# First block of a two-block model on one Trainium2 core: S5's scan in a rotating frame, TensorE's order given by a list, two sets of HGRN2 decay buffers

## Chip, core and metric

One core of a Trainium2 chip (trn2) runs the whole program in one launch. The metric is the device time of one execution in microseconds. Engines are named as in the profile: PE is TensorE (PEld its weight loads), DVE is VectorE, ACT is ScalarE, POOL is GpSimd, SP is SyncE, which here issues nearly all DMAs.

## The reference

Two transformer-like blocks on 1024 tokens of 1024 features; only the first is touched. It normalises x, multiplies by `w_in`, and splits the columns among four mixers; the mixers' outputs are concatenated, multiplied by `w_out`, and a feed-forward layer follows:

```
a = rms_norm(x); proj = a @ w_in            # 25 blocks of 128 columns
S5:    bu = u @ B;  x[t] = A*x[t-1] + bu[t] # complex, diagonal A, 16 groups x 64 states
       y = gelu(Re(C x) + d*u); y = y * sigmoid(y @ w_glu); rms_norm
HGRN2: b = cumsum(log f) per chunk; scores[t,s] = sum_k q k exp(b[t]-b[s])  (s <= t)
       o = (q exp(b)) @ state + scores @ v; state = exp(b_last)*state + (k exp(b_last-b))^T v
FoX:   softmax attention with a forget-gate bias
mLSTM: causal conv over q,k; gated matrix memory, chunk by chunk
h = x + rms_norm(concat(y) @ w_out); h = h + ffn(rms_norm(h)); block 2 ...
```

## The kernel before

All of it stands in `block1a` and its helpers. `norm_T` normalises x and puts it transposed into SBUF as a high and a low part (`a_hi`, `a_lo`). A projection of 128 columns loads 512 KB of weights, splits them into `wh`, `wl` (ACT L67, DVE L69) and, for each half of the tokens, runs 8 x 3 matmuls of 128x512 into one PSUM tile `g_ps` (`mm3`, L91 to L93). I call the 24 matmuls of one half a half; 25 projections (24 of 128 columns and the 12 gate columns) are 50 halves. `to_fm` copies a half out (ACT) and writes it to DRAM; `to_tm` also transposes it on PE first (`g_tp`, L196, copied by DVE L281). The mixers read their inputs back from DRAM.

S5 (`s5_prep`, `s5_main`) folds 8 tokens into one row, so 128 steps are left for each of 8 state tiles t. For each t, PE forms the drive (`w_ps`, L460), ACT copies it, and a scan by doubling runs 7 rounds; a round is three DVE operations (L468, L470, L471) and a POOL copy, each waiting for the last. Then PE forms the output (`y_ps`, L477 and L479) and ACT applies gelu. After all t come transposes (`gT_ps`), the gate product (`glu_ps`, L497) and the norm.

HGRN2 (`hg_main`) works in four quarters of 256 tokens. A quarter's decays are a chain over ACT (logs and exponentials, L564 on), DVE, and POOL (L592, L593: 14 differences for each of two feature halves f into the tile `hlev`), then ACT's exponential of `hlev` (L594) and DVE's products (L598, L600). Each quarter has two chunks of 128 tokens: scores on PE (`sc_ps`, L638), a mask on DVE (`hP`, L641), then `d_ps`, `o_ps` (L642 to L647) and the state's increment `st_ps` (L651) on PE; DVE updates the state (L655), and the output is transposed back (`oT_ps`, L664) and normed. `hlev`, `z`, `q` and most other decay tiles have one buffer, so the next quarter's `hlev` can't be written until this quarter's scores have read it. The values `hvc` of a chunk (two loads by SP, L627) have two buffers.

mLSTM's preparation (`ml_prep`: convolution and gate rows, nearly all DVE) starts when HGRN2's SBUF tiles are released; then `ml_chunk` and `fox_tile` alternate for 8 tiles. `fox_prep` needs the space of the activations `a_hi`, `a_lo`, so it follows the last projection.

The order of every engine's queue is made by a planner when the program is built: it plays the program through with its own costs and puts on each engine the first ready instruction in program order. So before the change projections fill PE wherever the planner believed a mixer to be waiting, in the order of `block1a`: u, z and q of HGRN2, `hv`, then S5 and HGRN2, then gate, mLSTM's and FoX's columns. On the chip a queue is kept in that order. Pools give SBUF space as a stack, and a tile in reused space waits for the tiles that lay there.

Of the kernel before, what the change touches and what calls it, by code (L numbers as in the profile page):

```python
# [10 lines left out]
F32 = mybir.dt.float32  # L11
FR = mybir.dt.float32r
BF = mybir.dt.bfloat16
# [7 lines left out]
P = 128  # L21
T = 1024
# [13 lines left out]
class Kern:  # L36
    def __init__(self, ctx, tc, ins, out, dbg=None):
        self.ctx, self.tc, self.nc = ctx, tc, tc.nc
        self.i = ins
        self.out = out  # L40
        self.dbg = dbg or (lambda *a: None)
        self.raws = 2
        self.wring = None


# [155 lines left out]
    def block1a(self, x, ymix):  # L201

        nc, tc, i = self.nc, self.tc, self.i
        with ExitStack() as st:
# [16 lines left out]
            with ExitStack() as gem, ExitStack() as s5:  # L221
                right = lambda name, bufs=1: pool(name, bufs, stack=gem, side="right")
# [5 lines left out]
                self.s5p = pool("s5p", stack=s5)  # L228
                with ExitStack() as t_:
                    tmp = pool("n_tmp", stack=t_)  # L230

                    def load(t):
                        xt = tmp.tile([P, D], F32, tag="x", name="xt", bufs=8)
                        nc.sync.dma_start(xt, x[t * P:(t + 1) * P, :])
                        return xt
                    self.norm_T(self.sm, self.pst, load, 0, *a, lambda: tmp.tile([P, D], F32, tag="sq", name="n_sq"))
                    for j in range(2):
                        self.to_tm(j * P, self.d_u, j * P)
                    for j in range(2):
                        self.to_fm(512 + j * P, self.d_hz[j])  # L240
                        self.to_fm(256 + j * P, self.d_hq[j])
                    for j in range(4):
                        self.to_tm(768 + j * P, self.d_hv, j * P)
                    self.s5_prep(tmp)
                with ExitStack() as h_:
                    self.s5_main(pool("s5m", stack=h_))
                    self.hg_main(pool("hg", stack=h_))
                    self.gate_gemm()
                    for j in range(4):
                        self.to_fm(2052 + j * P, self.d_mqk[j])  # L250
                    for j in range(4):
                        self.to_tm(2564 + j * P, self.d_mv, j * P)
                    for j in range(2):
                        self.to_fm(1280 + j * P, self.d_fq[j])
                        self.to_fm(1536 + j * P, self.d_fk[j])
                        self.to_tm(1792 + j * P, self.d_fv, j * P)

            mp = pool("ml")
            with ExitStack() as t_:
                self.ml_prep(mp, pool("mlt", stack=t_))  # L260
# [6 lines left out]
    def to_fm(self, c0, dst):  # L267
# [6 lines left out]
        self.gemm_fm(self.i["w_in"], c0, consume)  # L274

    def to_tm(self, c0, dst, d0):
# [6 lines left out]
        self.gemm_tm(self.i["w_in"], c0, P, consume)  # L283

    def gate_gemm(self):
# [8 lines left out]
        gb = self.sm.tile([12, 1], F32, name="gbias")  # L294
        nc.sync.dma_start(gb, dap(self.i["gate_bias"], 0, [[1, 12], [1, 1]]))

        def consume(h, ps):
            o = self.stg.tile([P, 512], F32, tag="gs", name="gs")
            nc.vector.tensor_scalar(o[0:12], ps, gb, None, op0=ALU.add)
            nc.sync.dma_start(self.d_gate[:, h * 512:h * 512 + 512], o[0:12])  # L300
        self.gemm_halves(wh, wl, 12, consume)


    def s5_prep(self, tmp):
# [35 lines left out]
        pr = mx.tile([P, 8, 8], F32, name="s5pr")  # L340
        pi = mx.tile([P, 8, 8], F32, name="s5pi")
        pn = mx.tile([P, 8, 8], F32, name="s5pn")
# [13 lines left out]
        r, m = ar, ai  # L356
        for j in range(10):
            r2 = tt(tt(r, r, M), tt(m, m, M), S)
            m2 = tt(r, m, M)
            V.tensor_scalar(m2, m2, 2.0, None, op0=M)  # L360
            r, m = r2, m2
            if j >= 2:
                if j - 2 < 7:
                    V.tensor_copy(pr[:, :, j - 2], r)
                    V.tensor_copy(pi[:, :, j - 2], m)
                    V.tensor_scalar(pn[:, :, j - 2], m, -1.0, None, op0=M)
        self.s5pw = (pr, pi, pn)
# [40 lines left out]
        gs = sm.tile([16, 16, P], F32, name="s5gs")  # L408
        for g4 in range(4):
            ps = self.pss.tile([P, 512], F32, tag="s", name="g_ps")  # L410
# [16 lines left out]
        BL = self.s5BL = mx.tile([P, 8, 2, P], F32, name="s5BL")  # L427
        for t in range(0, 8, 2):
# [6 lines left out]
        for k in range(2):  # L435
            nc.sync.dma_start(self.s5wg[k], i["s5_w_glu"][0, k * P:(k + 1) * P])

    def s5_main(self, mx):
        nc, sm = self.nc, mx
        V = nc.vector  # L440
        M, A = ALU.mult, ALU.add
# [3 lines left out]
        for c in range(2):  # L445
            nc.gpsimd.tensor_copy(u2[:, 8 * c:8 * c + 8], u[:, :, P * c:P * c + P].rearrange("b i (g p) -> b g i p", p=16))
        ub = mx.tile([P, 16, P], F32, tag="u", name="s5ub")
        for g4 in range(4):
            ps = self.pst.tile([P, 4, P], F32, tag="t", name="ub_ps")
            for j in range(4):  # L450
                nc.tensor.transpose(ps[:, j], u2[:, 4 * g4 + j].rearrange("b i p -> b (i p)"), self.ident)
            nc.scalar.copy(ub[:, 4 * g4:4 * g4 + 4], ps)
        gt = mx.tile([P, 8, 256], F32, tag="u2", name="s5g")
        pr, pi, pn = self.s5pw
        CA = self.s5CA
        for t in range(8):
# [5 lines left out]
            X = [sm.tile([P, 2, P + 1], F32, tag=f"u{j}", name=f"s5x{j}", bufs=2) for j in range(2)]  # L462
            nc.scalar.copy(X[0][:, :, 1:], ps)
            for j in range(7):
                d = 1 << j
                a, b = X[j % 2], X[(j + 1) % 2]
                e = P + 1 - d
                V.scalar_tensor_tensor(b[:, :, 1 + d:], a[:, :, 1:e], pr[:, t, j:j + 1], a[:, :, 1 + d:], op0=M, op1=A)  # L468
                nc.gpsimd.tensor_copy(b[:, :, 1:1 + d], a[:, :, 1:1 + d])
                V.scalar_tensor_tensor(b[:, 0, 1 + d:], a[:, 1, 1:e], pn[:, t, j:j + 1], b[:, 0, 1 + d:], op0=M, op1=A)  # L470
                V.scalar_tensor_tensor(b[:, 1, 1 + d:], a[:, 0, 1:e], pi[:, t, j:j + 1], b[:, 1, 1 + d:], op0=M, op1=A)  # L471
            X = X[1]
            nc.gpsimd.memset(X[:, :, 0:1], 0.0)
# [11 lines left out]
        for k in range(2):  # L485
            for i4 in range(2):
                ps = self.pst.tile([P, 4, P], F32, tag="t", name="gT_ps")
                for j in range(4):
                    nc.tensor.transpose(ps[:, j], gt[:, 4 * i4 + j, k * P:(k + 1) * P], self.ident)
                nc.scalar.copy(gT[:, k, 4 * i4:4 * i4 + 4], ps)  # L490
        y2 = gt
        ss = sm.tile([P, 8], F32, name="s5ss")
        for i2 in range(4):
            ps = self.pst.tile([P, 2, 256], F32, tag="t", name="glu_ps")
            for j in range(2):
                for k in range(2):
                    nc.tensor.matmul(ps[:, j], gT[:, k, 2 * i2 + j], self.s5wg[k], start=(k == 0), stop=(k == 1))  # L497
            th = sm.tile([P, 2, 256], F32, tag="th", name="s5th", bufs=2)
# [3 lines left out]
            for j in range(2):  # L502
                nc.scalar.activation(th[:, j], y2[:, 2 * i2 + j], AF.Square, accum_out=ss[:, 2 * i2 + j:2 * i2 + j + 1])
        r = self.mean_rstd(sm, ss, 8, 256, 4 * EPS)
# [6 lines left out]
    def hg_main(self, mx):  # L511
# [3 lines left out]
        L = P  # L515

        for l in range(7):
            h = 64 >> l
            nc.sync.dma_start(dap(self.d_hvc, l * 256, [[h * 1792, 512 // h], [1792, h], [1, 256]]),
                              dap(self.d_hv, 0, [[2 * h * 512, 512 // h], [512, h], [1, 256]]))  # L520
# [33 lines left out]
        W2 = 256  # L554
        for qt in range(T // W2):
            s0 = slice(qt * W2, (qt + 1) * W2)
            z = mx.tile([P, 2, W2], F32, tag="z", name="hz")
            q = mx.tile([P, 2, W2], F32, tag="q", name="hq")
# [1567 lines left out]
```

## Time and profile before

| | |
|---|---|
| Median of 3 runs | 2963.76 us (2963.69 to 2968.23) |
| Profiled execution | 2964.78 us, its span 2963.1 us |
| Mean granted PE clock | 0.951 of full speed |
| PE / PEld / DVE / ACT / POOL busy | 91% / 76% / 62% / 42% / 23% of the span |

PE is the busiest engine over the whole span, but a mean over stages says little about this one. The stages of the first block are told apart by where their tiles appear in time: up to 47 us constants and the norm with the first projections; to 200 us projections; to 321 us S5 among projections; to 488 us HGRN2's chunks among projections; to 564 us the remaining projections, with mLSTM's preparation on DVE; to 590 us the start of mLSTM and FoX; to 716 us both together. `PEclk` is the granted clock as a share of 2.4 GHz: 0.5 is 1.2 GHz, and a value between is a mixture over the stretch.

### The profile page before, as it was taken

To read this page: it belongs to the slowest core of one execution; us is meant where nothing else is said; L and a number is where in the kernel's file an instruction comes from. 1 tells how busy PE (TensorE), PEld (TensorE's weight loads), DVE (VectorE), ACT (ScalarE), POOL (GpSimd) and SP (SyncE) were. 2 spreads that over 40 slices of the span, in tenths; PEclk is the share of its full clock that TensorE was granted. 3 is DMA by queue.
4 is the path that set the end of the run, shared out by engine and by line. 5 is a ranking of instruction groups with operands and counts; after the bars stand their busy time and mean duration, and the time that the engine had idled before them with its cause. 6 is when DMAs were issued, how large, how long until landed. Compare 5 with 4: busy or idle time off the path is not lost. (4 is left out here: it accounts for less than half of the span.)

```text
span 2963.1 us, 45158 instructions
## 1 busy us (share of the span) xinstructions
PE 2693.6 (91%) x16614; PEld 2252.8 (76%) x16631; DVE 1840.0 (62%) x4486; ACT 1235.7 (42%) x2379; POOL 693.3 (23%) x848
## 2 busy tenths in 40 slices
PE   5977878898999999899999999999999999799894
PEld 4855556687799978899887787888887888587683
DVE  5137666677688975988755263566655265776565
ACT  3124343254344465444654153344333122455553
POOL 6002221000267730577202000000000010332221
PEclk9988877899999999999999999999999999899997
DMA  4242222423232324432346252621113455699995
GB/s 120 72 138 68 64 76 88 136 81 112 94 114 86 112 89 136 135 115 86 107 136 172 65 158 57 154 74 45 47 40 120 167 178 171 204 308 314 297 302 209
DMA packets 336050, 388.65 MB, mean 131 GB/s; under 512 B 46962, under 2 KB 276220, under 8 KB 335684
## 3 DMA queue, kind: packets, MB, share of 16 engines
q1 hardware_dynamic: 322404, 355.65, 38.9%
q0 software_dynamic: 13280, 29.58, 3.6%
q8 instruction: 132, 2.16, 0.3%
q14 instruction: 90, 0.74, 0.1%
q10 hardware_dynamic: 144, 0.52, 0.0%
HBM read 326.83 MB, written 79.77 MB: 137 GB/s over the span
## 5 line engine op out<-in xcount | busy, mean ns | idle before, releaser
L69 DVE TENSOR_TENSOR f_w<-f_wr,f_w 128x512 fp32r<-128x512 f32 x264 | 293.8, 1139 | 54.6 <-ACT f_w L67 53.2
L91 PE MATMUL g_ps<-a_hi,wh 128*128 128x512 f32 (+1 forms) x648 | 269.6, 416 | 2.5 <-ACT wh L67 1.4
L92 PE MATMUL g_ps<-a_lo,wh 128*128 128x512 f32 (+1 forms) x648 | 265.6, 410 | 0.0
L93 PE MATMUL g_ps<-a_hi,wl 128*128 128x512 f32 (+1 forms) x648 | 263.2, 407 | 0.0
L67 ACT ACTIVATE f_w<-f_wr 128x512 fp32r<-128x512 f32 x264 | 158.9, 624 | 178.7 <-POOL f_wr L1080 58.0
L91 PE MATMUL f_ps<-t,f_w 128*128 128x256 f32 x704 | 202.9, 288 | 14.6 <-DVE c L1064 11.5
L93 PE MATMUL f_ps<-t,f_w 128*128 128x256 f32 x704 | 202.2, 288 | 7.5 <-DVE f_w L69 7.3
L92 PE MATMUL f_ps<-t,f_w 128*128 128x256 f32 x704 | 200.2, 284 | 0.0
L1314 ACT ACTIVATE at_sb<-at_sb,at_m 128x256 f32<-128x256 f32 (+7 forms) x224 | 142.3, 636 | 131.8 <-DVE at_m L1312 57.4
L69 DVE TENSOR_TENSOR wl<-wr,wh 128x1024 fp32r<-128x1024 f32 (+1 forms) x61 | 74.0, 1213 | 167.6 <-ACT wh L67 167.4
L1545 POOL TENSOR_TENSOR o<-o,on 128x256 f32<-128x256 f32 x32 | 24.6, 769 | 623.2 <-DVE at_z L1334 294.8
L91 PE MATMUL e_gps<-e_wh,e_xTh 128*128 128x256 f32 x528 | 152.8, 289 | 0.0
L91 PE MATMUL f_ps<-b,f_w 128*128 128x256 f32 x528 | 149.9, 284 | 2.6 <-ACT f_w L67 1.3
L93 PE MATMUL f_ps<-b,f_w 128*128 128x256 f32 x528 | 149.5, 284 | 2.1 <-DVE f_w L69 2.1
L91 PEld LDWEIGHTS f_ps<-t,f_w 128*128 128x128 f32 x704 | 135.9, 193 | 19.1 <-issue 15.1
L92 PE MATMUL e_gps<-e_wl,e_xTh 128*128 128x256 f32 x528 | 149.7, 284 | 0.0
L93 PE MATMUL e_gps<-e_wh,e_xTl 128*128 128x256 f32 x528 | 149.6, 283 | 0.0
L92 PE MATMUL f_ps<-b,f_w 128*128 128x256 f32 x528 | 149.3, 283 | 0.0
L91 PEld LDWEIGHTS g_ps<-a_hi,wh 128*128 128x128 f32 (+1 forms) x648 | 125.5, 194 | 27.6 <-ACT a_hi L72 1.7
L93 PEld LDWEIGHTS f_ps<-t,f_w 128*128 128x128 f32 x704 | 136.0, 193 | 11.4 <-DVE f_w L69 11.3
L93 PEld LDWEIGHTS g_ps<-a_hi,wl 128*128 128x128 f32 (+1 forms) x648 | 124.4, 192 | 25.5 <-issue 0.2
L92 PEld LDWEIGHTS g_ps<-a_lo,wh 128*128 128x128 f32 (+1 forms) x648 | 125.2, 193 | 24.2 <-issue 0.2
(668 smaller groups left out, 7786.7 us busy)
## 6 DMA issues: line engine op xcount, KB each, us to landing
e_wg<-in_w_gate_e_dram SPq DMA_DIRECT2D x33, 1024.0 KB
e_wu<-in_w_up_e_dram SPq DMA_DIRECT2D x33, 1024.0 KB
e_wd<-in_w_down_e_dram SPq DMA_DIRECT2D x33, 1024.0 KB
wr<-in_w_in_dram SPq DMA_DIRECT2D x60, 512.0 KB
f_dr<-in_w_ffn_down_dram SPq DMA_DIRECT2D x52, 512.0 KB
f_wr<-in_w_ffn_gate_dram SPq DMA_DIRECT2D x44, 512.0 KB
f_wr<-in_w_ffn_up_dram SPq DMA_DIRECT2D x44, 512.0 KB
Q<-qd SPq DMA_DIRECT2D x64, 256.0 KB
```

The costliest lines, as they stand in the source:

```text
L67: a = self.nc.scalar.activation(hi, raw, AF.Copy)
L69: return a, (eng or self.nc.vector).tensor_tensor(lo, raw, hi.bitcast(F32), ALU.subtract)
L91: nc.tensor.matmul(ps, lh, rh, start=(j == 0), stop=False)
L92: nc.tensor.matmul(ps, lh, rl, start=False, stop=False)
L93: self.last_mm = nc.tensor.matmul(ps, ll, rh, start=False, stop=(j == n - 1))
L1314: nc.scalar.activation(p, p, AF.Exp, bias=m[:, hd:hd + 1], accum_out=z[:, hd:hd + 1])
L1545: nc.gpsimd.tensor_tensor(o4, o4, on, A)
```

## The change

It touches `block1a` alone. **Order of PE.** `seq()` ties each PE instruction of its block behind the last PE instruction of the block before, so PE's queue follows a written list; the other engines are still planned. `gemms` is a generator that issues one half of a projection at each `next`; the transposes of a `to_tm` half now follow one half later. **List.** z and q of HGRN2 come first (first half of the tokens for all four, then the second), then u and `hv` with S5's preparation between; then S5, with a half after each step while the second-last list has any (5 of the 11 steps); the 30 halves of gate, mLSTM and FoX go 3 into S5's tail, 20 into HGRN2's 8 chunks (after the scores one, or two in an odd chunk, and one after the products), 6 into `ml_prep` and 1 behind it. **S5.** Multiplying by powers of the conjugate phase turns the complex recurrence into two real ones with the real factor mag^8, done by one scan instruction each; a table `E` of cosines and sines is built in `s5_prep` by doubling (42 DVE operations), with a renormalised squaring (`unit`, `square`). The copy of the drive by ACT goes; the output of t is formed two steps after its state. **HGRN2.** The first quarter's decays are issued before S5, the next quarter's when a quarter begins, in turn in the pools `hg` and `hg2`; `hg2` lies where S5's tiles were. Chunks are split into scores, products and output; the output of a chunk comes after the scores of the next. `d_ps`, `st_ps` and `o_ps` share one PSUM bank; `hvc` now has one buffer. The norm's discarded squares are written as bf16.

```diff
+    @contextmanager
+    def seq(self):
+        with self.tc.issue_after(self.pe_last) if self.pe_last else nullcontext():
+            yield
+        ins = self.nc.cur_bb.bb.instructions
+        self.pe_last = next(i for i in reversed(ins) if i.engine == mybir.EngineType.PE)
...
+                            norm(0)
+                            fm = [(512, self.d_hz[0]), (640, self.d_hz[1]), (256, self.d_hq[0]), (384, self.d_hq[1])]
+                            w = [self.load_w(self.ws, i["w_in"], fm[j][0], P, raw_bufs=self.raws, ring=early if j < 2 else None)
+                                 for j in range(4)]
+                            norm(1)
+                            prep = self.s5_prep(right("s5t", stack=p_))
+                            next(prep)
+                            for h in range(2):
+                                for j in range(4):
+                                    with self.seq():
+                                        self.gemm_half(w[j], P, h, self.keep_fm(fm[j][1]))
+                        hga = pool("hg", stack=hg_)
+                        self.hg_setup(hga)
+                        quarters = [self.hg_quarter(0, hga)]
+                        g = self.gemms([("tm", 128 * j, self.d_u, 128 * j) for j in range(2)]
+                                       + [("tm", 768 + 128 * j, self.d_hv, 128 * j) for j in range(4)])
+                        for _ in range(4):
+                            next(g)
+                        for _ in range(3):
+                            with self.seq():
+                                next(prep)
+                            next(g)
+                    s5m = right("s5m", stack=s5)
+                    for step in self.s5_steps(s5m):
+                        next(g, None)
...
+                    for step in self.s5_tail(s5m):
+                        next(g)
+                with ExitStack() as b_:
+                    hgb = right("hg2", stack=b_)
+                    for c in range(NT):
+                        if c % 2 == 0 and c // 2 + 1 < 4:
+                            quarters.append(self.hg_quarter(c // 2 + 1, hgb if c // 2 % 2 == 0 else hga))
+                        d = quarters[c // 2]
+                        with self.seq():
+                            self.hg_scores(d, c)
+                        if c:
+                            with self.seq():
+                                self.hg_out(quarters[(c - 1) // 2], c - 1)
+                        next(g)
+                        if c % 2:
+                            next(g)
+                        with self.seq():
+                            self.hg_products(d, c)
+                        next(g)
...
-        r, m = ar, ai
-        for j in range(10):
-            r2 = tt(tt(r, r, M), tt(m, m, M), S)
-            m2 = tt(r, m, M)
-            V.tensor_scalar(m2, m2, 2.0, None, op0=M)
...
+        E = self.s5E = mx.tile([P, 2, 8, P], F32, name="s5E")
+        for j in range(7):
+            d = 1 << j
+            c0, s0, c1, s1 = (E[:, a, :, x * d:x * d + d] for x in range(2) for a in range(2))
+            br, bm = (a[:, :, None].to_broadcast([P, 8, d]) for a in (r, m))
+            t_ = te[:, :, 0:d]
+            V.tensor_tensor(c1, c0, br, M)
+            V.tensor_tensor(t_, s0, bm, M)
+            V.tensor_tensor(c1, c1, t_, S)
+            V.tensor_tensor(s1, c0, bm, M)
+            V.tensor_tensor(t_, s0, br, M)
+            V.tensor_tensor(s1, s1, t_, A)
...
-            nc.scalar.copy(X[0][:, :, 1:], ps)
-            for j in range(7):
-                V.scalar_tensor_tensor(b[:, :, 1 + d:], a[:, :, 1:e], pr[:, t, j:j + 1], a[:, :, 1 + d:], op0=M, op1=A)
-                nc.gpsimd.tensor_copy(b[:, :, 1:1 + d], a[:, :, 1:1 + d])
...
+            cs, sn = E[:, 0, t, None, :].to_broadcast([P, 2, P]), E[:, 1, t]
+            V.tensor_tensor(v, ps, cs, M)
+            V.tensor_tensor(w[:, 0], ps[:, 1], sn, M)
+            V.tensor_tensor(w[:, 1], ps[:, 0], sn, M)
+            V.tensor_tensor(v[:, 0], v[:, 0], w[:, 0], A)
+            V.tensor_tensor(v[:, 1], v[:, 1], w[:, 1], S)
+            for c in range(2):
+                V.tensor_tensor_scan(w[:, c], self.s5m8[:, t:t + 1].to_broadcast([P, P]), v[:, c], 0.0, M, A)
+            G.memset(X[:, :, 0:1], 0.0)
+            G.tensor_tensor(X[:, :, 1:], w, cs, M)
+            G.tensor_tensor(v[:, 0], w[:, 1], sn, M)
+            G.tensor_tensor(v[:, 1], w[:, 0], sn, M)
+            G.tensor_tensor(X[:, 0, 1:], X[:, 0, 1:], v[:, 0], S)
+            G.tensor_tensor(X[:, 1, 1:], X[:, 1, 1:], v[:, 1], A)
...
+        for t in range(10):
+            if t >= 2:
+                with self.seq():
+                    outputs(t - 2, X.pop(t - 2))
+            if t < 8:
+                with self.seq():
+                    X[t] = states(t)
+            yield
```

## Rows read from the trace of the kernel before

**Rows 1.** Busy time by stage: stretch, each engine's busy us, PEclk, DMA.
```profile
47.00:200.00 153.00, 142.77 (x675) 109.61 (x674) 29.36 (x48) 22.37 (x33) 28.22 (x69) 0.97 0.33 96
200.00:321.00 121.00, 84.53 (x574) 65.21 (x573) 83.46 (x227) 53.52 (x92) 26.59 (x92) 0.82 0.26 71
321.00:488.00 167.00, 128.71 (x1069) 91.46 (x1067) 102.60 (x348) 61.60 (x106) 47.95 (x98) 0.70 0.24 64
488.00:564.00 76.00, 72.48 (x343) 59.26 (x344) 51.26 (x56) 29.80 (x36) 0.55 (x1) 0.98 0.35 114
564.00:590.00 26.00, 17.75 (x127) 14.86 (x124) 17.63 (x64) 8.84 (x19) 1.30 (x4) 0.75 0.90 239
590.00:716.00 126.00, 115.56 (x837) 97.68 (x837) 94.07 (x454) 62.11 (x146) 3.66 (x10) 0.96 0.20 62
```

**Rows 2.** The same for the instructions on the projections' PSUM tile g_ps alone.
```profile
47.00:564.00 517.00, 312.44 (x1226) 224.12 (x1226) 4.18 (x6) 27.10 (x47) 0.85 0.29 82
```

**Rows 3.** PE in order of time: two projection matmuls.
```profile
83.66 0.39 PE L91 MATMUL g_ps<-a_hi,wh 128*128 128x512 f32 x1
...
89.10 0.39 PE L91 MATMUL g_ps<-a_hi,wh 128*128 128x512 f32 x1
```

**Rows 4.** Waits of PE, 0 to 860 us: us in total, times, longest.
```profile
PE y_ps L479 <- DVE s5x L470: 25.7, 7, 13.4
PE sc_ps L638 <- DVE hlev L600: 17.9, 11, 5.2
...
PE o_ps L643 <- DVE hqe L606: 12.7, 2, 7.0
```

**Rows 5.** DVE in order of time: first and last operation of one S5 state.
```profile
203.25 0.49 DVE L468 SCALAR_TENSOR_TENSOR s5x<-s5x,s5pr 128x254 f32<-128x254 f32 x1 [12.00 <-ACT s5x L463]
...
211.25 0.28 DVE L471 SCALAR_TENSOR_TENSOR s5x<-s5x,s5pi,s5x 128x64 f32<-128x64 f32 x1
```

**Rows 6.** DVE by line, to 600 us: count, busy us, mean ns.
```profile
L579 DVE TENSOR_TENSOR_SCAN hb<-ones,ht 128x128 f32<-128x128 f32 x16 | 8.0, 508 | 0.0
...
L316 DVE TENSOR_TENSOR s5s<-s5s,s5s 128x8 f32<-128x8 f32 x30 | 4.6, 176 | 3.2 <-ACT s5s L338 2.6 <-ACT s5s L339 0.5
...
L575 DVE TENSOR_TENSOR ht<-ht,ht 128x512 f32<-128x512 f32 x4 | 2.8, 690 | 0.8 <-ACT ht L573 0.8
```

**Rows 7.** POOL by line, to 600 us, same columns.
```profile
L593 POOL TENSOR_TENSOR hlev<-hb 128x128 f32<-128x128 f32 x56 | 27.4, 489 | 0.0
```

**Rows 8.** DVE in order of time: a decay product while POOL works, and later.
```profile
403.55 0.48 DVE L600 TENSOR_TENSOR hlev<-hlev,hq 128x128 f32<-128x128 f32 x1
...
407.07 0.28 DVE L600 TENSOR_TENSOR hlev<-hlev,hq 128x128 f32<-128x128 f32 x1
```

**Rows 9.** POOL in order of time: a difference alone, and one beside DVE.
```profile
400.47 0.40 POOL L592 TENSOR_TENSOR hlev<-hb 128x128 f32<-128x128 f32 x1
...
403.44 0.44 POOL L593 TENSOR_TENSOR hlev<-hb 128x128 f32<-128x128 f32 x1
```

**Rows 10.** ACT in order of time: first operation of the last quarter's decays.
```profile
419.42 0.63 ACT L564 ACTIVATE ht<-hz 128x512 f32<-128x512 f32 x1
```

**Rows 11.** DVE in order of time: that quarter's last product.
```profile
458.52 0.41 DVE L614 TENSOR_TENSOR hke<-hke,hz 128x256 f32<-128x256 f32 x1
```

**Rows 12.** DVE in order of time: first and last operation of mLSTM's preparation.
```profile
495.86 0.75 DVE L701 TENSOR_SCALAR mqk<-mraw,vcol 128x1024 f32<-128x1024 f32 x1 [4.32 <-DMA mraw<-fm_mqk]
...
544.42 0.68 DVE L742 TENSOR_SCALAR frow<-frow 4x1024 f32<-4x1024 f32 x1
```

**Rows 13.** PE in order of time: last transposes, mLSTM's first, FoX's first.
```profile
563.69 0.66 PE L196 MATMUL g_tp<-ident,g_raw 128*128 128x128 f32 x4 [0.68 <-ACT g_raw L193]
564.18 0.38 PE L782 MATMUL mk_ps<-ident,mqk 128*128 128x128 f32 x2
...
589.36 0.47 PE L866 MATMUL at_s<-fkA,f_Q 128*128 128x128 f32 x1 [5.84 <-ACT f_Q L860]
```

**Rows 14.** Busy time, columns as in rows 1, while two loads of hvc land.
```profile
383.00:389.00 6.00, 0.00 (x0) 0.00 (x0) 1.00 0.85 208
```

More of the change, by code (lines that the diff above doesn't have):

```diff
@@ L265, in block1a, with gemm_half, gemms, flip @@
                 self.fox_tile(t)
-    def to_fm(self, c0, dst):
+    def gemm_half(self, w, n, h, consume):
+        ps = self.psg.tile([P, 512], F32, tag="g", name="g_ps")
+        self.mm3(ps[0:n], [(w[0][:, k, 0:n], w[1][:, k, 0:n], *self.a_half[h][k]) for k in range(KT)])
+        consume(h, ps[0:n])
+    def gemms(self, specs):
+        nc = self.nc
+        load = lambda sp: self.gate_w() if sp[0] == "gate" else self.gemm_w(self.i["w_in"], sp[1])
+        ahead = load(specs[0])
+        turn = []
+        def flip(h, ps, dst, d0):
+            raw = self.stg.tile([P, 512], F32, tag="gm", name="g_raw")
+            nc.scalar.copy(raw, ps)
+            def later():
+                tp = self.psg.tile([P, 4, P], F32, tag="g", name="g_tp")
+                for j in range(4):
+                    nc.tensor.transpose(tp[:, j], raw[:, j * P:(j + 1) * P], self.ident)
+                self.keep_tm(dst, d0)(4 * h, tp)
+            turn.append(later)
+        for j, sp in enumerate(specs):
+            w = ahead
+            if j + 1 < len(specs):
+                ahead = load(specs[j + 1])
+            for h in range(2):
+                now, turn[:] = list(turn), []
+                with self.seq():
+                    if sp[0] == "tm":
+                        self.gemm_half(w, P, h, partial(flip, dst=sp[2], d0=sp[3]))
+                    elif sp[0] == "fm":
+                        self.gemm_half(w, P, h, self.keep_fm(sp[2]))
+                    else:
+                        self.gemm_half(w, 12, h, self.keep_gate)
+                for t in now:
+                    with self.seq():
+                        t()
+                if turn and j + 1 == len(specs) and h == 1:
+                    with self.seq():
+                        turn.pop()()
+                yield
+    def keep_fm(self, dst):
         nc = self.nc
@@ L494, in s5_main @@
             ps = self.pst.tile([P, 2, 256], F32, tag="t", name="glu_ps")
[L495 to L498, printed above, removed]
+            with self.seq():
+                for j in range(2):
+                    for k in range(2):
+                        nc.tensor.matmul(ps[:, j], gT[:, k, 2 * i2 + j], self.s5wg[k], start=(k == 0), stop=(k == 1))
+            th = sm.tile([P, 2, 256], F32, tag="th", name="s5th")
             nc.scalar.activation(th, ps, AF.Tanh, scale=0.5)
@@ L514, in hg_main @@
         M, A, S = ALU.mult, ALU.add, ALU.subtract
[L515 to L520, printed above, removed]
+        self.hsm = sm
         lm = sm.tile([P, 7, 64], BF, name="hmask")
@@ new lines, in hg_scores @@
+    def hg_scores(self, d, c):
+        nc, sm = self.nc, self.hsm
+        V = nc.vector
+        M = ALU.mult
+        cc = c % (self.W2 // P)
+        lm, lev = self.hg[0], d["lev"]
+        vg = sm.tile([P, 512], F32, tag="v2", name="hvg", bufs=2)
+        nc.sync.dma_start(vg, self.d_hv[c * P:(c + 1) * P, :])
+        vc = sm.tile([P, 7, 2, HD], F32, tag="hvc", name="hvc")
+        for b_ in range(2):
+            nc.sync.dma_start(vc[64 * b_:64 * b_ + 64].rearrange("s l f d -> s (l f) d"),
+                              dap(self.d_hvc, c * 64 * 1792 + b_ * HD, [[1792, 64], [P, 14], [1, HD]]))
+        kT = sm.tile([P, 2, P], F32, tag="u0", name="hkT", bufs=2)
+        ps = self.pst.tile([P, 2, P], F32, tag="t", name="kT_ps")
+        for f in range(2):
+            nc.tensor.transpose(ps[:, f], d["ke"][f][:, cc], self.ident)
+        nc.scalar.copy(kT, ps)
+        pms = []
+        for f in range(2):
+            sc = self.pss.tile([P, 7, 64], F32, tag="s", name="sc_ps")
+            for l in range(7):
+                for b_ in range(2):
+                    pq = slice(64 * b_, 64 * b_ + 64)
+                    nc.tensor.matmul(sc[pq, l], *[lev[f][pq, l, a, 64 * cc:64 * cc + 64] for a in range(2)],
+                                     start=True, stop=True)
+            pm = sm.tile([P, 7, 64], F32, tag="hP", name="hP", bufs=2)
+            V.tensor_tensor(pm, sc, lm, M)
+            pms.append(pm)
+        d[c] = vg, vc, kT, pms
@@ L743, in ml_prep @@
         nc.sync.dma_start(self.d_fF, Ff)
+        for _ in range(6):
+            next(g, None)
         cols = sm.tile([P, 4, NT, 4], F32, name="mcols")
```

434 lines of the change are left out of this document (234 added, 200 removed).

## The prediction

> **What bounds the kernel now.** I read the page's slices first: PE is busy nine tenths of the span, but the first block has slices with PE at 6 or 7 and a granted clock below full. Then the busy time by stage, because an average over the block would hide which recurrence costs what. Here the reader should multiply PE's busy time by the clock, which gives its work at full speed [rows 1]: 142.77 x 0.97 = 138 us of 153, 84.53 x 0.82 = 69 of 121, 128.71 x 0.70 = 90 of 167, 72.48 x 0.98 = 71 of 76. From 47 to 564 us that is 369 us of work in 517 us: 148 us are lost, 15 in the projections, 52 beside S5, 77 in HGRN2 and 5 at the end. An upper limit on the work is what this is, as a busy PE also holds the tails of matmuls; the 1226 matmuls of the projections [rows 2], less S5's 64 on a tile of the same name, take 1162 x 5.44/24 = 263 us of it at the pitch of one half [rows 3]. So PE is the bound wherever it has work it may start, and the loss is waiting plus what it costs in clock: 0.70 in HGRN2's stage is a mixture of 1.2 and 2.4 GHz.
>
> The waits of PE name the places [rows 4]: S5's output on DVE's scan (25.7 us), HGRN2's scores on the products that make `hlev` (17.9), its output on `hqe` (12.7). These sum to 56 us, so most of the 148 isn't a wait at a semaphore but matmuls at half rate after one, and recurrence work queued in small groups. DVE's order of time shows why S5 waits: one state takes from 203.25 to 211.5 us, 8.3 us in seven rounds [rows 5]. For HGRN2 a quarter's decays run from 419.42 to 458.9 us, 39 us from the first ACT operation to the last product [rows 10, 11], and they end after the quarter before has freed its only `hlev`.
>
> **The change part by part.** I sum what is still lost between 47 us and mLSTM's first matmul, now at 564.18 [rows 13], since the work of PE stays (the same matmuls and transposes, in another order).
>
> *Start.* S5's preparation drops 71 DVE operations of about 0.18 us and gains 99 such, plus 42 for the table E: six of each of seven widths from 8 to 512 elements, between 0.18 and 0.69 us [rows 6], about 2.1 us a set, 12.7 us. Net 17.5 us more on DVE, which has 29 us of work in the 153 us to 200 [rows 1]; that slack hides it, and E isn't needed before S5's first state. If the planner puts it ahead of the norm's evictions, PE pays it all: 0 to 17, I take 4. The drive of S5 now needs u back from DRAM in space that the preparation frees late; 0 to 6 behind one half of cover, I take 3. Together 7.
>
> *S5.* A state now costs DVE one product of 256 columns out of PSUM (between a 128- and a 512-wide one, 0.28 and 0.69 [rows 6, 8], I take 0.42), four operations at 0.28 and two scans at 0.51 [rows 6]: 2.5 us in place of 8.3. POOL gets five operations, four of 128 at 0.49 [rows 7] and one of twice that, 2.9 us, which did only small copies before. DVE, POOL and PE work on neighbouring t, so a step takes the longest, 2.9, and a little for the hops: 3.2 us. Five of the eleven steps have a half of 5.44 us behind them, which hides the chain. Six have none: 19 us, with 8 us of PE work in them, so 11 lost, 4 for the last state's way through DVE, POOL and PE, 5 for matmuls at 1.2 GHz during and after. 20 us; without clock loss and at DVE's 2.5 us a step it would be 8, at twice the step 40.
>
> *HGRN2.* A chunk holds 2.5 halves (13.6 us) and, by my estimate, 6 us of its own matmuls: of the 369 - 263 = 106 us that aren't projections, S5, its preparation and the transposes take about half, and 48 remain for eight chunks. Two chunks and the half before them are 45 us, against 39 us for a quarter's decays [rows 10, 11], which can now start while the last quarter is used. So the decays just fit, and between scores and products stands 5.4 or 10.9 us for DVE's mask. `hvc` loses its second buffer: two loads kept the DMA engines 0.85 busy over 6 us [rows 14], in a window of at least one half and the next scores, 8 us. That is hidden with 2 us to spare; without the cover it is 6 us a chunk. I take 10 us lost over the eight chunks, with 0 if all fits and 45 if three quarters come 15 us late. This is the main gain: 77 goes to 10.
>
> *Preparation of mLSTM.* Its DVE work spans 495.86 to 545.1 us, after 4.3 us of waiting for a load: 53.5 us [rows 12]. Before, PE had 72 us of work in that stage [rows 1]. The list leaves seven halves, 38 us, and 2 us of transposes. So 14 us of PE are bare, and 3 for the clock: 17; 8 if the loads find their space early, 30 if DVE is also late with HGRN2's output.
>
> The projections' order, the later transposes of `to_tm` and the bf16 squares I cost at nothing: PE has the next half meanwhile. SP issues the same loads and stores, in another order.
>
> *Sum.* 7 + 20 + 10 + 17 = 54 us lost where 148 are: mLSTM begins 94 us sooner. Beyond that point FoX waits for the last projection: 563.69 to 589.36 is 26 us [rows 13], in which PE did 17.75 x 0.75 = 13 us on mLSTM [rows 1]. Now the last projection ends 14 us before mLSTM begins instead of with it, so FoX starts 14 us sooner still, with some 7 us of mLSTM left over for the stage that PE fills at 0.96. I keep 4 of the 7 net: 98 us. The profiled execution took 2964.78, 1.0 more than the median: 2964.8 - 98 - 1 = 2866 us. With all lower bounds (16 lost) it is 132 + 6 = 138 us and 2825; with all upper ones (17 + 6 + 40 + 45 + 30 = 138) 10 us and 2953.
>
> **The rivals.** *POOL and DVE in each other's way.* A product of DVE takes 0.48 us while POOL works on its differences and 0.28 after [rows 8]; POOL's difference goes from 0.40 to 0.44 [rows 9]. S5's states now put long operations on both at once. If the two took strict turns, a step would be DVE's four operations with both inputs in SBUF, 1.6 us, plus POOL's 2.9: 4.5 in place of 3.2, six times, 8 us more: 2874. The Trainium skill (SBUF — State Buffer, Who interferes with whom) says just that: the two share one port pair under an exclusive lock. By that rule the loser waits for the other's whole instruction; the rows agree in direction, but DVE's 0.20 more is half of a POOL operation, and POOL hardly slows.
>
> *The ends show.* Both bare places at their upper bounds, S5's tail 40 and mLSTM's preparation 30, 33 us more: 2899. For it: DVE is what both wait on, and it has the quarter's decays beside. Against: DVE is busy only 83 of 121 and 103 of 167 us there now [rows 1], with 8 x 8.3 = 66 us of scan to drop for 20.
>
> *The second set doesn't work.* `hg2` lies on S5's tiles and the planner may still issue a quarter's decays after the chunk before; then HGRN2's 77 us stay, 67 more: 2933. For it: POOL and DVE are queues, and one decay that waits holds what stands behind. Against: the tiles no longer force it.
>
> *The list starves PE (slower).* In a planned queue a stalled product has projections in front; in a written one everything stands behind it. The place is `hg_products`: its mask waits on DVE, perhaps behind the 28 products of a quarter's `hlev`. If each of the eight chunks idles and then runs at half clock, 98 + 10 us are eaten at 13.5 us a chunk, and from there the change is slower; at 15 us it is 2866 + 110 = 2976. For it: the longest single waits are 5 to 7 us in HGRN2 [rows 4], yet its stage loses 77: waits are paid several times over in clock. Against: one half stands in each gap.
>
> **How the numbers follow.** Forecast 0.44; turns of POOL and DVE 0.12; the ends 0.16; the second set 0.12; starved 0.08; all bounds kind (about 2830) 0.08. 0.2% is 5.9 us, about what a measurement here can tell from no change. Faster holds all but the starved case and a little of the second set's upper end: 0.89; the same 0.03; slower 0.08. The range must reach from the kind case, most of it, to past the second set: 2830 to 2938, which leaves out the starved case and the edges, some 0.15.
>
> **What would show it.** Right: no POOL copy and no round of three in S5, a step of about 3 us; PE's clock near 1 from 47 us to the end of HGRN2 except in S5's last six steps; waits of the scores on `hlev` gone; mLSTM's first matmul near 470 us, with PE idle 10 to 20 us before it behind the gate rows. Wrong: waits of `o_ps` on the mask or on `hvc` in every chunk, a clock of 0.7 in HGRN2's stage, or a start of S5 much after 137 us, which is 47 + 13.4 halves (15 less those done) + 17 us for preparation and transposes.

## The result, and the profile after

| | before | changed |
|---|---|---|
| Median of 4 runs | 2965.99 us (2963.69 to 2968.75) | 2927.55 us (2922.52 to 2931.43) |
| Profiled execution | 2964.78 us | 2922.52 us, its span 2920.8 us |
| Mean granted PE clock | 0.951 | 0.957 |

The ratio is 0.9869 (95% interval 0.9849 to 0.9889): 38 us faster, inside the stated range of 2830 to 2938, but 61 us above the forecast of 2866, which had promised 98. mLSTM's first matmul came at 513.98 us and not near 470. The stages after, with bounds at the same events as before (S5's first transposes, HGRN2's first chunk, its last output, mLSTM's first matmul, the end of FoX); columns as in [rows 1]:

```profile
47.00:162.60 115.60, 91.29 (x447) 73.00 (x445) 59.38 (x161) 31.27 (x47) 44.32 (x101) 0.92 0.28 72
162.60:255.08 92.48, 87.94 (x440) 66.01 (x441) 28.24 (x83) 22.39 (x54) 21.17 (x47) 0.88 0.27 80
255.08:451.39 196.31, 170.20 (x1570) 142.67 (x1569) 116.42 (x335) 73.79 (x117) 44.55 (x95) 0.90 0.36 100
451.39:513.98 62.59, 47.98 (x221) 39.34 (x220) 50.02 (x68) 26.15 (x31) 1.59 (x4) 0.84 0.30 94
513.98:669.21 155.23, 138.80 (x931) 117.25 (x929) 105.42 (x497) 62.91 (x151) 4.98 (x14) 0.84 0.30 89
```

Length less busy time times clock, as in the prediction, gives what each stage lost: 31.6 us up to S5, 15.1 in S5, 43.1 in HGRN2 and 22.3 in mLSTM's preparation, 112 in all, where the forecast had 7, 20, 10 and 17. The measure is rough: HGRN2's 1570 matmuls count 153 us of work here and 162 in the run below with all orders mended, so 8 or 9 of its 43 us are the measure. What PE waited for between 47 and 520 us (columns as in [rows 4]):

```profile
PE o_ps L834 <- ACT hkT L805: 14.4, 2, 7.4
PE oT_ps L860 <- ACT hoS L847: 9.9, 1, 9.9
PE mc_ps L947 <- ACT mrow L923: 9.2, 1, 9.2
PE g_tp L341 <- ACT g_raw L336: 9.1, 3, 7.9
PE ub_ps L581 <- POOL s5u L575: 8.9, 1, 8.9
PE g_ps L100 <- ACT wh L76: 6.4, 1, 6.4
```

The old waits, on S5's scan, `hlev` and `hqe`, are gone. In their place PE waits for short copies on ACT, and a copy of 0.35 us can't take 7 us. What stood ahead of it shows on ACT in order of time (start, duration, line, operation, idle before and its releaser), in the third chunk of HGRN2; below it the instruction of PE that waited:

```profile
314.54 1.70 ACT L765 ACTIVATE hlev<-hlev 128x1792 f32<-128x1792 f32 x1 [4.62 <-POOL hlev L764]
316.15 0.57 ACT L370 COPY gs<-g_ps 128x512 f32<-128x512 f32 x1
320.04 1.70 ACT L765 ACTIVATE hlev<-hlev 128x1792 f32<-128x1792 f32 x1 [3.32 <-POOL hlev L764]
321.64 0.40 ACT L784 ACTIVATE hke<-hke 128x256 f32<-128x256 f32 x1
321.95 0.35 ACT L805 COPY hkT<-kT_ps 128x256 f32<-128x256 f32 x1
```
```profile
322.35 0.70 PE L834 MATMUL o_ps<-hvg,hkT 128*64 128x64 f32 x8 [6.98 <-ACT hkT L805]
```

The exponentials of the next quarter's `hlev` stand ahead of this chunk's `hkT`, and both wait for POOL's differences, the first and last of which are:

```profile
308.28 0.43 POOL L763 TENSOR_TENSOR hlev<-hb 128x128 f32<-128x128 f32 x1 [0.36 <-DVE hb L750]
...
319.56 0.44 POOL L764 TENSOR_TENSOR hlev<-hb 128x128 f32<-128x128 f32 x1
```

PE, which by the list may do nothing else, goes on with its products at 322.35, 7 us late, and needs 7.4 us for the rest of them, which takes 3.1 in the chunk before: 1.8 us more of waiting, for the mask, and a granted clock of 0.50 from 322.35 to 329.71. The next quarter's decays ended at 325 us; the scores that need them came at 359.4.

Ahead of S5 the same happens with quarter 0. DVE's copy of a mask waits for POOL, which makes the mask only after S5's tables; the weights' split on ACT stands behind the decays that stand behind that copy; later u's `g_raw` stands behind the exponentials; and S5's read of u is issued on SP behind the stores of `hv`. DVE, PE and SP in order of time:

```profile
85.83 0.27 DVE L693 COPY hmask<-hmask 64x448 bf16<-64x448 bf16 x1 [12.22 <-POOL hmask L691]
```
```profile
91.94 0.79 PE L100 MATMUL g_ps<-a_hi,wh 128*128 128x512 f32 x1 [6.42 <-ACT wh L76]
112.74 1.12 PE L341 MATMUL g_tp<-ident,g_raw 128*128 128x128 f32 x4 [7.87 <-ACT g_raw L336]
162.60 3.80 PE L581 MATMUL ub_ps<-ident,s5u 128*128 128x128 f32 x16 [8.87 <-POOL s5u L575]
```
```profile
147.49 7.37 SPq L380 DMA_DIRECT2D tm_hv<-gs  x2
155.50 0.62 SPq L572 DMA_DIRECT2D s5u<-tm_u  x1
```

### The profile page after: what moved, and what is told of

Its sections match the earlier page's. It is cut to its first block, busy times and chain, and to the rows that moved or that the text cites. A ratio compares the mean times of both kernels' runs of the same rounds, so it can differ in the third digit from the quotient of the medians.

```text
span 2920.8 us, 45015 instructions
## 1 busy us (share of the span) xinstructions
PE 2665.4 (91%) x16614; PEld 2252.0 (77%) x16631; DVE 1835.7 (63%) x4446; ACT 1221.4 (42%) x2361; POOL 698.4 (24%) x832
## 5 line engine op out<-in xcount | busy, mean ns | idle before, releaser
L100 PE MATMUL f_ps<-t,f_w 128*128 128x256 f32 x704 | 203.1, 289 | 15.5 <-DVE c L1262 12.6
L100 PEld LDWEIGHTS f_ps<-t,f_w 128*128 128x128 f32 x704 | 136.6, 194 | 19.7 <-issue 16.2
L102 PEld LDWEIGHTS f_ps<-t,f_w 128*128 128x128 f32 x704 | 136.6, 194 | 9.2 <-DVE f_w L78 9.1
```

Source lines behind the costliest of these rows:

```text
L100: nc.tensor.matmul(ps, lh, rh, start=(j == 0), stop=False)
L102: self.last_mm = nc.tensor.matmul(ps, ll, rh, start=False, stop=(j == n - 1))
```

## The experiments

Ratios are to the kernel before on the same chip, with 95% intervals; the changed kernel is 0.9869. 0.001 is 3 us.

**The exponentials behind the copies.** `levels` holds L765 to L771; `act_last()` is here the copy `hoS`.

```diff
                             self.hg_products(d, c)
+                        if c % 2 == 0 and c // 2 + 1 < 4:
+                            with tc.issue_after(self.act_last()):
+                                quarters[c // 2 + 1]["levels"]()
```

> The changed kernel with one difference in order: in quarters 1 to 3 of HGRN2 the two exponentials of hlev on ACT, and the products behind them, are issued behind the copy hoS of the running chunk; POOL's 28 differences stay where they are. Theory A (ACT's queue: the exponentials, put early by the planner, wait for POOL's differences and hold the copies hkT and hoS that PE needs): the three waits of PE in HGRN2's stage (9.9, 7.0 and 7.4 us) go with the half clock behind them, the stage falls from 196 to about 165 us and the time from 2927.6 to about 2895. Rival B (a quarter's decays are simply too long beside two chunks): the scores of the next quarter now wait for hlev, and the time stays within 6 us of 2927.6 or grows. Rival C (the clock stays low for another reason): the waits go but the clock of the stage stays at 0.90, and only about 24 us are won.

0.9783 (0.9766 to 0.9799), 25 us less than the changed kernel. HGRN2 took 171.3 us in place of 196.3, at a clock of 0.98:

```profile
257.78:429.06 171.28, 163.73 (x1570) 137.15 (x1569) 116.79 (x335) 72.82 (x117) 46.84 (x95) 0.98 0.41 114
```

Its waits on `hkT` are gone; one on `hoS`, of 6.7 us, is left, on a state update that stood on DVE behind a decay (L753 of that kernel) waiting for ACT. Only the exponentials and DVE's products behind them were moved, and POOL's differences kept their place, so theory A holds: not the length of a quarter's decays but their place in the queue was the cost.

**The start.** Three edits ahead of S5; `act_last()` is here the copy of u's third half.

```diff
-        V.tensor_copy(lm[64:128], lm[0:64])
+        G.tensor_copy(lm[64:128], lm[0:64])
...
+                                with tc.issue_after(self.act_last()):
+                                    quarters[0]["levels"]()
...
-        nc.sync.dma_start(u, self.d_u.rearrange("(b i) f -> b i f", i=8))
+        nc.gpsimd.dma_start(u, self.d_u.rearrange("(b i) f -> b i f", i=8))
```

> The changed kernel with three edits ahead of S5: the copy of HGRN2's mask is done by POOL instead of DVE; the exponentials of quarter 0's hlev are issued on ACT behind the copy of u's third half; S5's u is read back through POOL's queue instead of SP's. Theory A (queues in a fixed order hold PE's inputs behind HGRN2's early decays): the waits of PE of 6.4 us (wh) and 7.9 us (g_raw) go, that of 8.9 us on s5u falls to about 4, S5's transposes begin at about 140 instead of 162.6 us, and the time falls by about 20 to 2907. Rival B (S5's start is set by S5's own preparation on POOL and DVE): the transposes begin no earlier than 157 and the time stays within 6 us.

0.9763 (0.9745 to 0.9781), 31 us less. S5's transposes began at 137.03 in place of 162.60, the time that the prediction had worked out for a start without loss, and from 47 us to there PE lost 2 us. What each of the three edits brought isn't separated:

```profile
47.00:137.03 90.03, 88.12 (x448) 71.53 (x447) 57.58 (x161) 31.70 (x47) 48.28 (x102) 1.00 0.33 89
```

**The halves of mLSTM's preparation first.** The loop of six halves in `ml_prep` moves from behind the gate rows to ahead of them.

> The changed kernel with one move: the six halves of ml_prep are issued in the program ahead of the gate rows instead of behind them. Theory A (the sixth half began, waited for its weights' low part, which stood on DVE behind the gate rows, and the transposes of the gate rows were queued inside it, so 46 of its and its successor's matmuls ran after them): the last projection ends near 493 us instead of 512, mLSTM's first matmul is near 500 instead of 514, FoX starts as much sooner, and the time falls by about 14 to 2913. Rival B (DVE's chain of 45 us from 458.9 is the bound whatever PE does): mLSTM begins no more than 4 us sooner and the time stays within 6 us.

0.9853 (0.9837 to 0.987), not told apart from the changed kernel. The last projection ended at 491 in place of 513, but mLSTM's gate columns were still complete only at 506.3 (498 in the changed kernel, which then had nearly two halves to do): DVE's chain takes some 45 us from 460 in either. Mostly rival B.

**One set of decay buffers.** `hgb` becomes `hga` in the list.

> The changed kernel with all quarters of HGRN2 in one set of decay buffers (hg2 is not used). A quarter's decays took 27 us in the changed kernel (255.8 to 282.5) and can now start only when the scores and products of the quarter before are done, with some 20 us of PE work up to the next scores. If the second set works (theory A): three waits of the scores on hlev of 7 to 15 us come, with half clock behind them, and the time grows by 20 to 45 us to 2948 to 2973. If it gives nothing because the copies on ACT are what PE waits for (rival B): within 6 us of 2927.6.

0.9912 (0.9896 to 0.9929), 13 us more: below theory A's 20, but not nothing. HGRN2 took 211 us. The waits on ACT's copies are gone from its rows, and the old ones are back:

```profile
PE sc_ps L812 <- DVE hlev L771: 22.5, 15, 5.9
PE kT_ps L804 <- DVE hke L785: 9.0, 3, 3.5
```

So the second set does what it says; it traded one wait for another.

**No list.** `seq()` yields without its tie.

> The changed kernel without the ties on PE: the same program, but TensorE's queue is ordered by the planner as on the other engines. Theory A (the list is worth something: it spreads the halves over S5 and HGRN2, and what was lost was lost to the other engines' queues): slower than the changed kernel by 15 to 40 us, ratio 0.992 to 1.000, with a clock near 0.8 or less in HGRN2's stage. Rival D (the list starves PE, as one of the rivals of the prediction had it: behind a stalled product everything stands): faster than the changed kernel by 10 us or more, ratio 0.9835 or less.

0.9766 (0.9747 to 0.9784): 30 us *faster* than with the list. I had expected the opposite. HGRN2 began at 237.5 us (255.1 in the changed kernel) and took 190.6 (196.3). Up to S5's transposes, S5, HGRN2:

```profile
47.00:174.21 127.21, 112.66 (x550) 90.78 (x549) 61.87 (x162) 34.74 (x52) 44.97 (x101) 0.95 0.29 76
174.21:237.47 63.26, 60.76 (x345) 42.84 (x343) 25.72 (x79) 18.31 (x49) 19.30 (x46) 0.97 0.26 80
237.47:428.03 190.56, 171.02 (x1564) 141.75 (x1563) 115.39 (x335) 71.81 (x116) 45.27 (x95) 0.93 0.39 108
```

The planner put whole halves in front of S5 and single projection matmuls between its steps. Three drives in a row there, 3.5 us apart at full clock (first fence), and those of the changed kernel's bare steps (steps with no half behind them), 3.1, 4.2 and 6.2 us apart:

```profile
201.06 0.66 PE L589 MATMUL w_ps<-s5ub,s5BL 128*64 128x128 f32 x8
204.65 0.66 PE L589 MATMUL w_ps<-s5ub,s5BL 128*64 128x128 f32 x8
208.06 0.66 PE L589 MATMUL w_ps<-s5ub,s5BL 128*64 128x128 f32 x8
```
```profile
206.75 0.66 PE L592 MATMUL w_ps<-s5ub,s5BL 128*64 128x128 f32 x8
209.88 0.66 PE L592 MATMUL w_ps<-s5ub,s5BL 128*64 128x128 f32 x8
214.09 0.66 PE L592 MATMUL w_ps<-s5ub,s5BL 128*64 128x128 f32 x8
220.25 1.12 PE L592 MATMUL w_ps<-s5ub,s5BL 128*64 128x128 f32 x8 [0.37 <-ACT s5g L621]
```

**S5's scan alone, in the kernel before.** The new table and states and outputs of S5 in the old `s5_prep` and `s5_main`, no list.

> The kernel before with the new S5 alone: table E and the rotating scan on DVE and POOL in place of the doubling rounds, outputs two steps later, nothing else of the change (to make room, hvc and the gate hth of HGRN2 have one buffer, the row of ones is one column, and S5's temporaries share a tag). Theory A (S5's scan was what PE waited for beside S5): the waits on s5x of 25.7 us go, a state takes about 3 us in place of 8.3, and the time falls by 15 to 30 us against the kernel before, ratio 0.990 to 0.995. Rival B (without a list the planner leaves S5 or HGRN2 bare in other places): ratio 0.998 or above.

1.0023 (1.0006 to 1.0039): nothing won. A state is short now, and S5's transposes of the output began at 250 in place of 312 us, HGRN2 ended at 446 in place of 485; yet mLSTM began at 564.5, as before:

```profile
201.80:257.11 55.31, 44.32 (x195) 33.05 (x194) 24.05 (x69) 30.46 (x45) 25.58 (x56) 0.57 0.17 48
257.11:446.00 188.89, 155.32 (x1291) 108.25 (x1291) 121.43 (x376) 76.29 (x134) 55.25 (x117) 0.74 0.26 74
446.00:564.50 118.50, 109.77 (x505) 88.31 (x505) 59.09 (x73) 36.46 (x46) 0.65 (x2) 0.97 0.32 100
```

The last row says where the gain went: the projections that had run beside the long scan were still to be done, 118 us of them, behind HGRN2. S5's stage (clock 0.57) and HGRN2's (0.74) still lost 30 and 74 us by the measure above. That smaller buffers in HGRN2 cost a part isn't excluded.

**All together.** The edits of the first three experiments, and a quarter's decays issued on ACT and DVE behind the chunk before (its copy `hoS` and its state update):

```diff
+                            with tc.issue_after(ends[0]) if c else nullcontext(), tc.issue_after(ends[1]) if c else nullcontext():
+                                quarters.append(self.hg_quarter(c // 2 + 1, ...
...
+                        ends = [self.last(e) for e in (mybir.EngineType.Activation, mybir.EngineType.DVE)]
```

> The changed kernel with the three edits together (exponentials of hlev behind hoS; the three edits ahead of S5; the halves of ml_prep ahead of the gate rows) and one more: a quarter's decays are issued on ACT and DVE behind the hoS copy and the state update of the chunk before, because with the first edit alone one wait of 6.7 us was left, on a state update that stood on DVE behind a decay that waited for ACT. Measured alone against the kernel before: ratios 0.9783, 0.9763, 0.9853, the changed kernel 0.9869. Theory A (each is a separate wait in a fixed queue): the gains add, 25 + 31 + 5 + 8 = 69 us less than the changed kernel, ratio 0.964, and no wait of PE in HGRN2's stage is over 2 us. Rival B (they share a bound behind them, DVE's chain in mLSTM's preparation): not more than 45 us less, ratio 0.972 or above.

0.9645 (0.9629 to 0.9661), 2857 us: the gains add, and no wait of PE in HGRN2's stage is over 2 us. Start, S5, HGRN2 and mLSTM's preparation:

```profile
47.00:137.50 90.50, 87.46 (x446) 71.18 (x445) 56.56 (x158) 27.89 (x42) 48.35 (x103) 1.00 0.33 89
137.50:230.62 93.12, 88.54 (x441) 66.46 (x441) 28.21 (x83) 22.21 (x54) 21.18 (x47) 0.87 0.29 82
230.62:397.61 166.99, 163.37 (x1570) 137.19 (x1569) 118.67 (x336) 66.48 (x114) 47.76 (x95) 0.99 0.43 117
397.61:453.11 55.50, 44.80 (x223) 37.15 (x222) 49.29 (x65) 28.83 (x35) 1.59 (x4) 0.90 0.41 116
```

**Halves moved from HGRN2 to S5**, on top of these edits (one list, a half behind all eleven steps, 13 in HGRN2, 7 in `ml_prep`).

> As e7_all, with the written list changed: one list of projections, a half behind each of the eleven S5 steps (five before), HGRN2's chunks get 13 halves in place of 20, ml_prep 7 in place of 6, one behind it as before. Theory A (six bare S5 steps lose about 14 us with their half clock, and mLSTM's preparation is DVE's chain, so a half moved into either place is free): about 15 us less than e7_all, ratio 0.959 if that one reaches 0.964. Rival B (a quarter's decays need some 33 us of two chunks, which then hold 33 us of PE work): scores wait for hlev or the output for ACT in three quarters, and it is no faster than e7_all.

0.9655 (0.9632 to 0.9678): no gain, rival B. S5 ran at a clock of 1.00 from 136.6 to 232 us, but HGRN2 with seven halves (40 us) less took 147.5 us, only 19.5 less, and waits on `hoS` (11.8 us in two) and on the mask (5.2) are back. A quarter then took 37 us (147.5/4); that its decays need as much is argued from this, not measured.

**Free on PE, with the edits of all together.** First all of PE, then S5's steps and tail alone; without its tie `seq()` only yields. The edit of the second, which ties PE again at HGRN2:

```diff
+                    self.tied = False
                     for step in self.s5_steps(s5m):
```

> e7_all without the ties on PE: the planner orders TensorE's queue, the four edits on ACT, DVE, POOL and SP's side stay. In e5_no_list S5 ran 177 to 214 us at full clock, with single projection matmuls between the steps, and a step took 3.4 us; in e7_all it ran 147 to 203 with six bare steps at half clock. Theory D (a whole half is too coarse a unit of cover; the planner's interleaving of single matmuls is worth 10 to 18 us even when the copies no longer wait): ratio 0.958 to 0.961. Rival A (once the copies on ACT no longer wait, the written list is as good): 0.9645 within 0.002, or slower, since HGRN2 in e7_all has no wait over 2 us and the planner put some there in e5_no_list.

> e7_all with the ties on PE lifted from S5's steps and tail alone (the halves issued there are free too); HGRN2 and all else stay tied. If the list's cost is the bare S5 steps and its gain is HGRN2's order, this is the best of the kernels: ratio 0.958 to 0.961, S5 without half clock and HGRN2 without a wait over 2 us. If free halves in S5 only move the bare place (behind the list in HGRN2 the same number of halves is left): 0.9645 within 0.002.

0.9614 (0.9596 to 0.9631) and 0.961 (0.9593 to 0.9626). The tie costs about 10 us in S5 and nothing that shows in HGRN2 once the copies don't wait.

**S5 free in the changed kernel.**

> The changed kernel with that one edit: the ties on PE lifted from S5's steps and tail, all else as changed. e5_no_list was 0.9766 against 0.9869; its profile had S5's gate products done 18 us sooner and HGRN2's end 6 us sooner still. If most of what the ties cost lies in S5 (the wait of 8.9 us on s5u and the bare steps): ratio 0.980 to 0.983, with HGRN2's three waits on ACT's copies as in the changed kernel. If it lies in HGRN2: 0.985 or above.

0.9825 (0.9809 to 0.9842), 13 us less. HGRN2 began at 237.7, as without any list (237.5), but took 203 us against 190.6: with the copies waiting, the tie cost there too.

**Two halves moved to mLSTM's preparation**, from the best of these (18 in HGRN2, 8 in `ml_prep`).

> e11_s5_free with two of HGRN2's 20 halves moved into ml_prep (8 in place of 6, one behind it as before). In e11 the projections ended at 430 us and mLSTM's preparation, bound by DVE's chain that begins when HGRN2 ends (391), left PE 15 us with little work and half clock until 450 and after. Theory A (that bare place is real, the halves in HGRN2 are not all needed): HGRN2 ends 11 us sooner, mLSTM begins 8 to 11 us sooner, ratio 0.957 to 0.958. Rival B (a quarter's decays need some 36 us of two chunks, and two quarters now have 36): scores or outputs wait again in two quarters, 5 to 10 us each, and the ratio stays at 0.961 within 0.002.

0.9597 (0.9577 to 0.9617), 2846.55 us: the lowest, not told apart from 0.961. mLSTM's gate columns came 8 us sooner (437 for 445), and FoX's end 9, though waits on the mask (6.3 us in three) came with it; 6 of the 9 were lost later in the program, where the runs don't say why.

## Why the prediction was wrong

The direction and the range held; the size was off by 61 us, and the sum by stage says where. Against the forecast, mLSTM began 44 us late: 24.6 at the start, 33.1 in HGRN2, 5.3 in its own preparation, less 4.9 in S5 and less 14 because the same work, counted as busy time times clock, came out smaller (355 for 369 us); those 14 are the measure, so the start and HGRN2 lost somewhat less than these terms say. Beyond mLSTM's start 15.5 us more went (11.5 lost where 4 were to be kept).

*Start, 4 + 3 us: this step failed.* Its first half had the size by luck: the first transposes of the norm came at 23.9 us instead of 17.95, and by 47 us PE was 3 us behind, but not because of table E, whose first operation ran at 33.58. SP now issues two loads of weights ahead of x, so x lands later and ACT squares it 4 us later (before; then changed); two more splits of weights on DVE, 1.22 us each, stand ahead of x's scaling:

```profile
8.25 1.06 ACT L104 ACTIVATE n_sq<-xt 128x1024 f32<-128x1024 f32 x1 [1.49 <-DMA xt<-in_x_dram]
```
```profile
12.29 1.06 ACT L113 ACTIVATE n_sq<-xt 128x1024 bf16<-128x1024 f32 x1 [0.36 <-DMA xt<-in_x_dram]
33.58 0.17 DVE L484 TENSOR_TENSOR s5E<-s5E,s5q 128x8 f32<-128x8 f32 x1
```

The second half was mis-sized because I asked only when S5's inputs come free. The new work in front of S5 that costs is quarter 0's decays: each of their waits on POOL holds ACT and DVE, and with these the weights and u. With the queues' order mended S5 began at 137.0, as computed. "SP issues the same loads and stores, in another order" was put at nothing, and both halves show it was not: the weights ahead of x, and u read behind the stores of `hv`.

*HGRN2, 10 us: this is the term that failed most.* "So the decays just fit" was right, with time to spare (325 for 359 us). The loss comes from a queue that the step never priced: ACT, which also carries `hkT`, `hoS`, `g_raw` and the weights, waits inside the decays for 28 differences of POOL, 12 us. Three quarters, three waits of 7 to 10 us, each with half clock behind it: by the times of the matmuls behind them they cost 10 to 13 us each, 35 of the 43; the other 8 or 9 are the measure. With all orders mended the stage lost 5 us (166.99 - 163.37 x 0.99, the third row of all together).

*S5, 20 us:* 15 measured. The step of 3.2 us was 3.5 where single matmuls lay between and 3.1 to 6.2 bare; the longest held 1.6 us of waiting and PE's matmuls at half rate. By the terms of its own sum the lower bound is 15 - 8 + 4 = 11 us and not 8. Strict turns of POOL and DVE did not come: a DVE operation took 0.53 us beside POOL's 0.50 and 0.28 alone, a state 1.9 us on DVE and 2.3 on POOL.

```profile
211.65 0.50 POOL L608 TENSOR_TENSOR s5x<-s5x,s5v 128x128 f32<-128x128 f32 x1
211.76 0.53 DVE L601 TENSOR_TENSOR s5v<-s5v,s5w 128x128 f32<-128x128 f32 x1
```

By the exclusive lock of the Trainium skill (SBUF — State Buffer, Who interferes with whom) the loser would wait for all of the other's turn; 0.25 more is half of one, as before [rows 8, 9].

*mLSTM's preparation, 17 us:* 22 measured. But FoX was to start 14 us sooner still, since the last projection would end early. It ended at 512.75. The list does not reach `ml_prep`'s own transposes (they are not tied): the planner put them inside the sixth half, whose low weights stood on DVE behind the whole chain:

```profile
497.48 1.21 DVE L78 TENSOR_TENSOR wl<-wr,wh 128x1024 fp32r<-128x1024 f32 x1
```
```profile
479.33 0.40 PE L101 MATMUL g_ps<-a_lo,wh 128*128 128x512 f32 x1
...
494.61 1.86 PE L947 MATMUL mc_ps<-ident,mrow 4*128 4x4 f32 x16 [9.20 <-ACT mrow L923]
...
498.74 0.80 PE L102 MATMUL g_ps<-a_hi,wl 128*128 128x512 f32 x1
```

The 4 us to be kept beyond mLSTM's start turned into 11.5 lost: mLSTM and FoX took 155.2 us for 143.75. PE was idle as long in both, 16.4 and 15.2 us; the rest is the clock, 0.84 and 0.92. The six kernels with the halves of `ml_prep` where the change has them took 150.9 to 155.2, and S5's scan alone, which from mLSTM on runs the program of before, took 150.7 (the kernel before, and that experiment, from mLSTM's first matmul to FoX's end):

```profile
564.18:707.93 143.75, 128.58 (x930) 108.99 (x929) 104.67 (x497) 63.62 (x151) 4.96 (x14) 0.92 0.33 93
```
```profile
564.53:715.18 150.65, 136.71 (x930) 115.23 (x929) 104.83 (x497) 63.44 (x151) 4.96 (x14) 0.86 0.31 89
```

So up to 7 of the 11.5 us come without the changed order of the projections; what lowers the clock there stays open.

*The rivals.* "The list starves PE" (0.08) had the kind of cause and the wrong queue: a stalled product with everything behind it, but held by copies on ACT, three times and not eight, 10 to 13 us each with the half clock, and by S5's bare steps. Without the list the change would have been worth 69 us, not 38. I gave it little weight because I looked for waits that a new instruction would *have*, and not for instructions queued behind one. "The second set doesn't work" came nearest in time (2933 for 2928), by luck: the set works (one set costs 13 us more). But what spoke for it, a decay that waits and holds what stands behind, was the mechanism, on ACT where it named POOL and DVE. "The ends show" (2899) was wrong: S5 lost 15 and not 40, the preparation 22 and not 30. With the orders mended the kernel takes 2857 us, and 2848 with S5 free: the forecast of 2866 was near that of the change without the queues.

## What to carry to other kernels

When work is issued earlier, list for each engine what stands behind its waits, short copies that feed another engine above all; that it ends in time is not enough. A hand-written order for one engine takes away its freedom to fill, so it is only as good as the queues of the others, and a unit of cover should be no larger than the gap. Shortening a chain beside which PE had other work moves that work and not the end (1.0023).

## What was unexpected on the chip

Waits cost more than they last. HGRN2's three waits of 7 to 10 us were each followed by a stretch at 1.2 GHz (6 to 8 us in which a projection matmul took 0.63 us or more for 0.39), so 24 us of waiting made the stage 29 us longer than with the orders mended (196.3 and 167.0). And S5's small matmuls, with single large ones between them, ran at a granted clock of 0.95 over 37 us in the kernel without the list, where the bare steps of the changed kernel had 0.69 (that the large ones do it is argued; nothing else was held equal):

```profile
177.00:214.00 37.00, 34.69 (x214) 24.66 (x213) 19.23 (x60) 7.98 (x20) 19.30 (x46) 0.95 0.15 41
```
```profile
204.70:231.30 26.60, 23.02 (x123) 17.53 (x121) 9.62 (x31) 4.89 (x15) 9.69 (x24) 0.69 0.39 119
```
